# A channel shuffle on one core: the second tile cut from 8 to 4 KB a partition, the last raised from 16 to 20

## The chip, the cores and the metric

The kernel runs on one core of a Trainium2 chip. The metric is the device time of one execution in microseconds; lower is better. The time before is the median of three runs.

## The reference

The input is a float32 array of 16 x 64 x 64 x 256. The 256 channels of each pixel form 8 groups of 32. The output holds the same numbers with the two indices of the channel exchanged:

```python
def reference(x, groups):
    batch, h, w, c = x.shape
    channels_per_group = c // groups
    x = x.reshape(batch, h, w, groups, channels_per_group)
    x = x.transpose(0, 1, 2, 4, 3)
    return x.reshape(batch, h, w, c).astype(np.float32)
```

Nothing is calculated. Each pixel is one row of 256 x 4 bytes = 1 KB, read once, permuted inside the row, and written once: 67.11 MB in and 67.11 MB out.

## The kernel before, in words

The 65,536 rows are cut along the pixels into 15 slots, listed in `_SLOTS` (line 12). A slot is one input tile and one output tile in SBUF, with 128 partitions. The number in the list is the count of rows that each partition holds; a row is 1 KB, so the number is also the KB a partition. The first slot is cut once more, into two pieces of 4 and 8 rows, which share the slot's two buffers and are loaded, permuted and stored apart from each other. In this text each piece is called a tile: the first has 4 KB a partition, the second 8, the third 28, then come twelve of 38, and the last has 16. The sum is 512 rows a partition, times 128 partitions.

All buffers have the size of the biggest slot, 38 KB a partition. There are two input buffers (`_IN_BUFS`, line 13) and three output buffers (`_OUT_BUFS`, line 14), used in turn by slots.

For each slot three things happen, in program order:

- Line 55: SyncE (SP in the profile) issues a DMA for each piece, from HBM to the input tile. Partition p gets a contiguous stretch of rows, so one partition's part is one contiguous run on both sides. A load waits until the copies that read its buffer two slots earlier are over. The profile calls SP's queue q1.
- Line 57: VectorE (DVE) copies each piece from the input tile to the output tile. The permutation is in the access pattern: `(i g j)` is read as `(i j g)`. A copy waits for its load, and for the stores of the slot three before it, which hold the output buffer.
- Line 61: ScalarE's queue (ACT) issues the store of each piece after its copy. The profile calls this queue q10. ScalarE calculates nothing.

The schedule is manual, so each engine's instructions stand in the order in which the loop writes them. Nothing else is on the three queues. TensorE is not used, and GpSimd only sets four constants at the start.

Of the kernel before, what the change touches and what calls it, by code (L numbers as in the profile page):

```python
# [1 line left out]

# [4 lines left out]


F32 = mybir.dt.float32
P = 128  # L10

_SLOTS = [[4, 8], [28]] + [[38]] * 12 + [[16]]
_IN_BUFS = 2
_OUT_BUFS = 3


@with_exitstack
def kernel(
    ctx: ExitStack,
    tc: tile.TileContext,  # L20
    x: bass.AP,
    groups: bass.AP,
    out: bass.AP,
):
    nc = tc.nc
    b, h, w, c = x.shape
    G = int(groups)
    CPG = c // G
    assert G * CPG == c
    assert sum(map(sum, _SLOTS)) * P == b * h * w  # L30
    biggest = max(map(sum, _SLOTS))

    x_flat = x.rearrange("b h w c -> (b h w c)")
    out_flat = out.rearrange("b h w c -> (b h w c)")

    in_pool = ctx.enter_context(tc.tile_pool(name="in_pool", bufs=_IN_BUFS))
    out_pool = ctx.enter_context(tc.tile_pool(name="out_pool", bufs=_OUT_BUFS))

    def rows(flat, first, q):

        return flat[first * c : (first + P * q) * c].rearrange("(p f) -> p f", p=P)

    ctx.enter_context(tc.manual_schedule(engines=None))
    first = 0
    for parts in _SLOTS:
        in_tile = in_pool.tile([P, biggest * c], F32, name="in_tile")
        out_tile = out_pool.tile([P, biggest * c], F32, name="out_tile")
        at = 0
        pieces = []
        for q in parts:  # L50
            pieces.append((q, first, slice(at * c, (at + q) * c)))
            first += P * q
            at += q
        for q, start, cols in pieces:
            nc.sync.dma_start(out=in_tile[:, cols], in_=rows(x_flat, start, q))  # L55
        for q, start, cols in pieces:
            nc.vector.tensor_copy(  # L57
                out=out_tile[:, cols].rearrange("p (i j g) -> p i j g", j=CPG, g=G),
                in_=in_tile[:, cols].rearrange("p (i g j) -> p i j g", g=G, j=CPG),
            )  # L60
            nc.scalar.dma_start(
                out=rows(out_flat, start, q), in_=out_tile[:, cols]
            )


# [1 line left out]
_INS = ['x', 'groups']  # L67
_OUTS = [((16, 64, 64, 256), 'float32')]

_NUMBERS = {'groups': 8}  # L70


# [26 lines left out]
```

## Time and profile before

| What | Value |
|---|---|
| Time, median of 3 runs | 316.07 us (316.06 to 316.1) |
| Span of the profiled execution | 314.4 us |
| VectorE: 16 copies | 119.0 us |
| VectorE idle ahead of its copies, put down to loads | 179.4 us |
| A copy of 38 KB a partition | 8.79 us (x12) |
| Copies of 4, 8, 16, 28 KB a partition | 1.09, 2.02, 3.87, 6.57 us |
| DMA packets | 4608, in 32 DMAs |

The profile is of one execution. Its span runs from the first to the last instruction on the core; the times of the runs also hold what lies around it. "DMA packets" are the records of the 16 DMA engines: each packet is one piece of a transfer on one engine. A queue's share of 16 engines is the time its packets took, summed, over 16 times the span or the stretch asked for. Because loads and stores run on the same 16 engines, the two queues' shares add up, and a sum near 100% says that the engines have no free time.

The profile lists a DMA's time from issue to landing. It contains the time that the DMA stood behind others in its queue, so it is not the time of the transfer itself: the twelve loads of 38 KB a partition took a median of 37.0 us each and the stores 42.6, although together they pass in less than 314 us.

### The profile page before, as it was taken

How to read it: one execution, taken by the hardware profiler on the slowest of the kernel's cores; microseconds unless marked ns; L12 is line 12 of the kernel's file. 1: busy time of each engine (PE TensorE's matmuls, PEld its weight loads, DVE VectorE, ACT ScalarE, POOL GpSimd, SP SyncE). 2: the span in 40 equal slices, each digit the busy share in tenths (PEclk: the TensorE clock that was granted, in tenths of full speed). 3: DMA queues.
4: the chain of work that ended last, by engine and by line, in shares of the span. 5: the costliest groups of instructions: out<-in, count | busy, mean ns of one | idle time of the engine just before them, and what ended most of it. 6: DMA issues, size and time to landing. Idle time of an engine off the chain costs nothing.

```text
span 314.4 us, 132 instructions
## 1 busy us (share of the span) xinstructions
DVE 119.0 (38%) x16; POOL 0.2 (0%) x4
## 2 busy tenths in 40 slices
DVE  2081907309109109019028028037046055065400
POOL 0000000000000000000000000000000000000000
DMA  7999999999999999999999999999999999999997
GB/s 317 405 441 416 435 416 483 401 465 406 450 421 446 426 436 436 401 470 396 475 396 475 396 470 401 470 401 470 401 450 421 446 426 436 436 417 450 429 421 321
DMA packets 4608, 134.22 MB, mean 427 GB/s; under 512 B 512, under 2 KB 512, under 8 KB 768
## 3 DMA queue, kind: packets, MB, share of 16 engines
q1 hardware_dynamic: 2304, 67.11, 49.8%
q10 hardware_dynamic: 2304, 67.11, 49.4%
HBM read 67.11 MB, written 67.11 MB: 427 GB/s over the span
## 4 chain that ended last, share of the span: by engine, by line
DMA 76%; DVE 19%; issue 0%; SPq 0%; DVEq 0%
DMA in_tile<-in_x_dram 76%; DVE out_tile L57 19%; SPq L55 0%; DVEq L57 0%
## 5 line engine op out<-in xcount | busy, mean ns | idle before, releaser
L57 DVE COPY out_tile<-in_tile 128x9728 f32<-128x9728 f32 (+4 forms) x16 | 119.0, 7440 | 179.4 <-DMA in_tile<-in_x_dram 179.4
L80 POOL MEMSET const-uint8-127<- 128x1 uint8 x1 | 0.1, 103 | 0.0
L80 POOL MEMSET const-bfloat16-1.0<- 128x1 bf16 x1 | 0.1, 102 | 0.0
L80 POOL MEMSET const-float32-1.0<- 128x1 f32 x1 | 0.1, 100 | 0.0
L80 POOL MEMSET const-float32-0.0<- 128x1 f32 x1 | 0.1, 99 | 0.2 <-issue 0.2
## 6 DMA issues: line engine op xcount, KB each, us to landing
in_tile<-in_x_dram SPq DMA_DIRECT2D x12, 4864.0 KB, 37.0
out_dram<-out_tile ACTq DMA_DIRECT2D x12, 4864.0 KB, 42.6
in_tile<-in_x_dram SPq DMA_DIRECT2D x1, 3584.0 KB, 14.7
out_dram<-out_tile ACTq DMA_DIRECT2D x1, 3584.0 KB, 30.9
in_tile<-in_x_dram SPq DMA_DIRECT2D x1, 2048.0 KB, 30.4
out_dram<-out_tile ACTq DMA_DIRECT2D x1, 2048.0 KB, 15.2
in_tile<-in_x_dram SPq DMA_DIRECT2D x1, 1024.0 KB, 5.4
out_dram<-out_tile ACTq DMA_DIRECT2D x1, 1024.0 KB, 25.0
```

The costliest lines, as they stand in the source:

```text
L57: nc.vector.tensor_copy(out=out_tile[:, cols].rearrange("p (i j g) -> p i j g", j=CPG, g=G), in_=in_tile[:, cols].rearrange("p (i g j) -> ...
L80: nc = _bacc.Bacc("TRN2", target_bir_lowering=False, num_devices=1)
```

## The change

The second tile gets 4 rows a partition in place of 8, and the last tile 20 in place of 16. The sum stays 512, and every tile in between keeps its size but begins 4 x 128 rows earlier in the arrays.

```diff
-_SLOTS = [[4, 8], [28]] + [[38]] * 12 + [[16]]
+_SLOTS = [[4, 4], [28]] + [[38]] * 12 + [[20]]
```

The number of loads, copies and stores, their order on each engine and the buffers stay as they are. The second copy has 128 x 1024 elements in place of 128 x 2048, and the last one 128 x 5120 in place of 128 x 4096.

## The prediction

> **What bounds the kernel now.** I read the page's table of slices and its list of queues first, because the page shows only two consumers of time, VectorE copies and DMA.
>
> ```profile
> span 314.4 us, 132 instructions
> DVE 119.0 (38%) x16; POOL 0.2 (0%) x4
> ...
> DMA  7999999999999999999999999999999999999997
> ...
> DMA packets 4608, 134.22 MB, mean 427 GB/s; under 512 B 512, under 2 KB 512, under 8 KB 768
> ...
> q1 hardware_dynamic: 2304, 67.11, 49.8%
> q10 hardware_dynamic: 2304, 67.11, 49.4%
> ```
>
> The DMA row holds a 9 in 38 of 40 slices, with a 7 at either end; VectorE works 38% of the span. The two queues (q1 carries the loads that SP issues, q10 the stores that ACT issues) keep the 16 DMA engines busy for 49.8 + 49.4 = 99.2% of the span: 0.992 x 314.4 = 311.9 us. Only 2.5 us are not packets. So the sum is one over packets, not over waits.
>
> The chain of waits tells another story at first sight, and it is the trap of this page:
>
> ```profile
> 264.01 30.41 DMA in_tile<-in_x_dram
> 294.42 0.03 issue
> 294.45 0.05 DVEq L57
> 294.50 0.04 issue
> 294.54 3.87 DVE out_tile L57
> ```
>
> These rows (start, length, what) end at 298.4 with the last copy, 16 us short of the span's end, as if load, copy and store of the last tile stood in line. The listing does not show the stores that were already queued. The issue list, asked between 270 and 290 us, gives the next-to-last store: issued at 286.96, 21.8 us to landing, so landed at 308.8. The last store, issued at 298.45, had to stand behind it on the same queue and landed 15.2 us after issue, at 313.6. Its copy was over some 10 us before its turn came.
>
> Where are the 2.5 us without packets? I cut the span into stretches (the columns: stretch, length, VectorE, GpSimd, TensorE clock, DMA share, GB/s):
>
> ```profile
> 0.00:2.00 2.00, 0.00 (x0) 0.20 (x4) 1.00 0.18 23
> ...
> 16.00:32.00 16.00, 8.39 (x2) 0.00 (x0) 1.00 1.00 425
> 32.00:36.00 4.00, 4.00 (x1) 0.00 (x0) 1.00 1.01 397
> ...
> 100.00:250.00 150.00, 55.91 (x7) 0.00 (x0) 1.00 1.00 432
> ...
> 312.00:314.40 2.40, 0.00 (x0) 0.00 (x0) 1.00 0.27 116
> ```
>
> The first 2 us hold 0.18 of a full DMA, so 1.6 us are empty; the last 2.4 hold 0.27, so 1.75 are empty. (Together a little over 2.5, because the packets' recorded times overlap a little elsewhere: shares of 1.01 and more.) In between there is no gap, only two rough stretches, 16 to 36 us, where the rate is 425 and 397 in place of 432.
>
> **The change part by part.** The counts stand: 16 loads, 16 copies, 16 stores, the same 67.11 MB each way. A queue's 2304 packets are 16 DMAs x 16 engines x 9, and the 512 packets under 512 B are 32 DMAs x 16 engines; so on each engine a DMA is 8 data packets, one for each of its 8 partitions, and one tiny one. The second tile's packets go from 8 KB to 4 KB, the last one's from 16 to 20 KB. Prices of a packet come from stretches in which one kind is alone on a queue (packets, MB, share of 16 engines):
>
> ```profile
> q1 hardware_dynamic: 70, 0.29, 100.2%
> ```
>
> between 2.6 and 3.3 us, all 4 KB: 0.7 x 16 x 1.002 / 70 = 0.1603 us.
>
> ```profile
> q10 hardware_dynamic: 112, 0.92, 19.7%
> ```
>
> between 20 and 31 us, all 8 KB: 11 x 16 x 0.197 / 112 = 0.3096 us.
>
> ```profile
> q10 hardware_dynamic: 80, 1.31, 101.8%
> ```
>
> between 309 and 312 us, all 16 KB: 3 x 16 x 1.018 / 80 = 0.6108 us. The trace has no 20 KB packet. From 4 to 16 KB a KB costs (0.6108 - 0.1603) / 12 = 0.0375 us; from 16 to 38 KB it is nearly the same: between 100 and 200 us the queues hold 100.7% with 1247 - 128 = 1119 data packets, 100 x 16 x 1.007 / 1119 = 1.440, and (1.440 - 0.6108) / 22 = 0.0377. So 20 KB: 0.6108 + 4 x 0.0376 = 0.761 us, whichever slope one takes.
>
> Removed on each queue: 8 x (0.3096 + 0.6108) = 7.363 us. Added: 8 x (0.1603 + 0.761) = 7.370 us. Over two queues the change costs +0.01 us. If I take 8 KB from the loads alone between 3.9 and 5.8 us (97 packets at 101.0%, 0.3165 us, cut packets at the edges counted whole), it is 2 x 8 x -0.007 = -0.10 us. I take the first price, and keep -0.10 to +0.01.
>
> Small transfers: the row above has 4 KB packets back to back, at 100.2% of the engines and 0.1603 us each, which is what the sum uses. A rule speaks against the change: the Trainium skill, DMA: Bandwidth & Descriptors, section Bandwidth, says to batch DMAs to at least 1 MiB, and the change halves a DMA of exactly 1 MiB. By the fixed 2.0 us plus bytes over 436 GB/s in that page's section Anatomy of one DMA, an estimate gives 4.4 us for the second load before and 3.2 after, 6.8 and 8.0 for the last one: again a sum of zero, since the number of DMAs stands; only a reading in which the 2.0 us are newly exposed would make it cost.
>
> Start, step by step. SP issues three loads with no wait, at 0.73, 1.15 and about 1.6 us. The second is 8 x (0.3096 - 0.1603) = 1.19 us shorter, so its copy starts at 6.61 - 1.19 = 5.42 (the first copy ends at 5.15), takes 1.09 as the first one does in place of 2.02, and ends at 6.51 in place of 8.63. The second store on ACT and the fourth load on SP go out 2.1 us earlier; SP and ACT have nothing else queued behind these than the next load and store. All this is worth nothing: the load queue is full without the fourth load until the third lands at 16.34 (now 15.15), and the stores that start earlier take turns from loads. The cover is the third load's 28 KB packets; without it the 2.1 us would be a gain.
>
> The third load's packets must be there 1.19 us earlier. The first load's packets start between 1.7 and 1.8 us, 1.0 after its issue; so the third's are due at about 2.6, and are wanted when the second load is done, about 4.7 on the earliest engine. Cost 0. The upper bound is the slowest case the trace has: the first store was issued at 5.19 and its first packet is seen between 9.0 and 9.2 us, 3.9 later, though behind the loads' packets. At that delay the third load would begin at 5.5, a hole of up to 0.8 us. I take 0, the case of an issue on an empty queue.
>
> Buffers. The copy of each tile also waits for the store three tiles back. All 179.4 us of idle VectorE are put down to loads; the first tile's stores land at 8.66 + 25.0 = 33.7, and the copy that reuses their buffer starts at 49.11. 15 us cover it; nothing moves by more than 2.1. Loads: SP issues each one when a copy ends (57.9, for one), some 13 us before the load in front lands (71.2).
>
> End. The last load starts 1.19 us earlier and is 8 x 0.150 = 1.20 longer, so it lands at 294.4 as before. VectorE: the copy of 16 KB a partition takes 3.87, and 4 KB more cost 2.02 - 1.09 = 0.93; so 4.80, and the store is issued at 299.4 in place of 298.45. The next-to-last store is now done at about 308.8 - 1.2 = 307.6. With 1.0 us from issue to first packet that leaves 7 us where 9 stood; the copy's 0.93 is hidden. The last store drains 8 x 0.761 = 6.09 in place of 4.89, 1.20 later, which is what the queue in front gave up.
>
> Sum: 314.4 + 0.01 = 314.4 for the span; the runs' median is 316.07, 1.6 above the profiled span, and that offset (launch and end outside the span) has no cause to move. 316.07 + 0.01 = 316.1 us.
>
> **Rivals.** (1) Tail exposed, slower. If the chain of waits were right, the last tile would stand alone: +0.93 of copy and +1.20 of drain: 316.07 + 2.13 = 318.2. It decides once the last store comes to its queue after the one in front is done. For it: that the chain ends there. Against it: 7 us of slack. 2 in 100.
>
> (2) Hole at the start, slower. The third load's packets come later than 3.1 us after their issue (1.6 + 3.1 = 4.7): up to 0.8 us, 316.9. For it: the 3.9 us of the first store. Against it: 1.0 us of the first load. 7 in 100, of which half passes 0.2%.
>
> (3) Smoother start, faster. The rough stretches cost 16 x (432 - 425)/432 = 0.26 and 4 x (432 - 397)/432 = 0.32 us. The second store's 8 KB packets lie in the first of them; were both to go with the smaller packets, 316.07 - 0.58 - 0.10 = 315.4. For it: from 36 us on the rate is full. Against it: 4 KB packets are dearer for each byte, and the loads beside the second store are the same. 6 in 100. The opposite, a new slow stretch of that size somewhere, gives 316.6; another 4 in 100.
>
> (4) Shorter fill, faster. If the first stores were what the end waits for, 2.1 us earlier gives 314.0. Against it: DMA is full from 2 us on. 1 in 100.
>
> **How the numbers follow.** No change, 316.1 with its own range 315.8 to 316.4 (-0.10 and half of the rough 0.58 either way): 80 in 100. The runs of before differ by 0.04 us; 0.2%, 0.63 us, is what I take as the least a measurement can tell. Slower by more: (1), half of (2) and a little of the opposite of (3): 0.07. Faster by more: (4), half of (3), rounded up: 0.05. Within: 0.88. The range for 8 in 10 reaches to the far side of (3) and most of (2): 315.4 to 316.8.
>
> **What would show it.** Queue shares that again sum to about 99.2%; second copy at 5.4 us with 1.09, last one 4.8 long with its store issued near 299.4 and 14 us to landing; an unbroken row of 9s. Wrong if a stretch near 4 to 6 us has a share well under 1 (rival 2), if stores' queue is empty between 300 and 309 (rival 1), or if the stretch from 100 to 250 us leaves 432 GB/s: then packets do not cost what their size says.

## The result, and the profile after

The changed kernel is slower: 318.07 us (median of 9 runs, 316.79 to 319.72) against 316.10 for the kernel before (9 runs in turn with them, 316.05 to 316.75). The ratio is 1.0054, with a 95% interval of 1.0035 to 1.0073. That is outside the predicted range, and on the other side of 0.2%. The spread is new too: the runs of before lie within 0.7 us, those of the changed kernel within 2.9. (Medians here are over all runs; ratios leave out executions over 1.5% above the fastest of the same kernel, and so do the readings of profiles below, which is why two of the experiments, e1 and g1, have none.)

The page of the changed kernel, of an execution that took 318.74 us, to be laid beside the lines that the prediction showed:

```profile
span 317.0 us, 132 instructions
...
DMA  8999999999999999999999999999999999999995
...
DMA packets 4608, 134.22 MB, mean 423 GB/s; under 512 B 512, under 2 KB 512, under 8 KB 1024
...
q1 hardware_dynamic: 2304, 67.11, 49.5%
q10 hardware_dynamic: 2304, 67.11, 49.0%
```

The packets and bytes are as many as before, and 256 more packets are under 8 KB: the second tile's. Their time is (0.495 + 0.490) x 317.0 = 312.2 us of 16 engines, against 311.9 before. So the packets cost 0.3 us more (0.4 when their recorded times are summed one by one, 312.40 against 311.99), and the span grew by 2.6. The DMA row has 9s in 38 slices, and the last digit has gone from 7 to 5.

The stretches at the end (stretch, length, VectorE, GpSimd, clock, DMA share, GB/s), first of the kernel before, then of the changed one:

```profile
312.00:313.30 1.30, 0.00 (x0) 0.00 (x0) 1.00 0.51 214
313.30:314.40 1.10, 0.00 (x0) 0.00 (x0) 1.00 0.00 0
```

```profile
312.00:313.80 1.80, 0.00 (x0) 0.00 (x0) 1.00 0.59 250
313.80:316.20 2.40, 0.00 (x0) 0.00 (x0) 1.00 0.04 17
```

In the changed kernel 2.4 us follow in which the share is 0.04, less than 1/16 = 0.06. The DMA view of 314.1 to 316.5 us says what moves there (40 slices: busy tenths, then GB/s):

```profile
DMA  0007000000000007000000000000000000000000
GB/s 0 0 0 341 0 0 0 0 0 0 0 0 0 0 0 341 0 0 0 0 0 0 0 0 0 0 0 0 0 0 0 0 0 0 0 0 0 0 0 0
DMA packets 3, 0.04 MB, mean 17 GB/s; under 512 B 1, under 2 KB 1, under 8 KB 1
```

Three packets one behind the other: two of 20 KB and a tiny one. That is a single engine, which finishes its share of the last store alone. The trace's landings, one for each engine, agree: the last store lands on 15 engines between 313.25 and 313.97 us, and on the sixteenth at 316.15. Before, all 16 land between 313.21 and 313.62. So of the 2.53 us between the two last landings, 316.15 - 313.97 = 2.2 are one engine's lateness and 0.35 are the other fifteen.

How it began can be read from the third copy. In the timeline (start, length, what, idle time before it) of the changed kernel:

```profile
16.34 6.56 DVE L57 COPY out_tile<-in_tile 128x7168 f32<-128x7168 f32 x1 [9.99 <-DMA in_tile<-in_x_dram]
```

It starts at 16.34, as it did before (16.36), although there are 4 KB less to load ahead of it; the prediction had its load landing at 15.15. The landings say why: on the first engine the third load is there at 14.86, on the last at 16.32, 1.46 us apart. Before they were 0.42 apart (15.92 to 16.34). A copy waits for the last of 16.

The lateness is there from the first packet of that load. On the engine that later ends alone it starts between 5.1 and 5.2 us, and no other packet starts in that stretch (packets, MB, share of 16 engines):

```profile
q1 hardware_dynamic: 1, 0.03, 146.8%
```

A packet counts with its whole time where it starts, so this one took 0.1 x 16 x 1.468 = 2.35 us, where a 28 KB packet usually takes 1.06. The first packets of seven other engines took 0.26 to 0.89 us too long, those of the remaining eight none. The first store's packets begin at 9.4 us, so no store was in the way.

The difference lasts. The DMA view of 100 to 112 us, before and after:

```profile
DMA  0295008920099000990009800292009920099000
GB/s 0 130 1686 259 0 0 389 1556 130 0 0 1297 778 0 0 0 1297 778 0 0 0 1686 389 0 0 130 1816 130 0 0 1038 908 130 0 0 1297 778 0 0 0
```

```profile
DMA  9025993099920989209892099039990299902989
GB/s 1167 0 130 259 778 908 130 0 519 519 908 130 0 778 389 778 130 0 778 389 778 130 0 778 1167 0 130 519 519 908 0 130 519 649 778 0 130 778 389 778
```

A packet is counted where it starts. Before, the 16 engines start theirs in clumps 1.44 us apart, the length of a 38 KB packet, with nothing between: all load, then all store. After, the clumps are smeared, and some engines load while others store. I call the state of before "in step". (For single engines I linked each packet record to the one that starts where it ends.)

### The profile page after: what moved, and what is told of

It reads as the page before. It is cut to its first block, busy times and chain, and to the rows that moved or that the text cites. A ratio compares the mean times of both kernels' runs of the same rounds, so it can differ in the third digit from the quotient of the medians.

```text
span 317.0 us, 132 instructions
## 1 busy us (share of the span) xinstructions
DVE 120.1 (38%) x16; POOL 0.2 (0%) x4
## 2 busy tenths in 40 slices
DMA packets 4608, 134.22 MB, mean 423 GB/s; under 512 B 512, under 2 KB 512, under 8 KB 1024
## 4 chain that ended last, share of the span: by engine, by line
DMA 76%; DVE 19%; issue 0%; SPq 0%; DVEq 0%
DMA in_tile<-in_x_dram 76%; DVE out_tile L57 19%; SPq L55 0%; DVEq L57 0%
## 5 line engine op out<-in xcount | busy, mean ns | idle before, releaser
L57 DVE COPY out_tile<-in_tile 128x9728 f32<-128x9728 f32 (+3 forms) x16 | 120.1, 7504 | 180.6 <-DMA in_tile<-in_x_dram 180.5
```

The lines of the kernel that those rows point to most:

```text
L57: nc.vector.tensor_copy(out=out_tile[:, cols].rearrange("p (i j g) -> p i j g", j=CPG, g=G), in_=in_tile[:, cols].rearrange("p (i g j) -> ...
```

## The experiments

Two theories at the start. A: the third load's packets, wanted 1.2 us earlier, come apart on the engines at the start. B: the 20 KB tile at the end makes the late engine. A third one, C, puts it on the shifted rows. The first four kernels change only the list of tiles.

```diff
-_SLOTS = [[4, 4], [28]] + [[38]] * 12 + [[20]]
+_SLOTS = [[4, 4], [32]] + [[38]] * 12 + [[16]]    e1_start
+_SLOTS = [[4, 8], [24]] + [[38]] * 12 + [[20]]    e2_end
+_SLOTS = [[4, 6], [28]] + [[38]] * 12 + [[18]]    e3_mid
+_SLOTS = [[12], [28]] + [[38]] * 12 + [[16]]      e4_single
```

> Only the second tile goes from 8 to 4 KB a partition; the third takes the 4 KB (32), the last stays at 16. Theory A (the loss comes from the start: the third load's packets begin at 4.7 us in place of 5.9, are slow there, and one DMA engine falls out of step and ends alone some 2 us after the others): slower like the changed kernel, 317 to 319 us with runs over 1 us apart, and a last engine alone after the others. Theory B (the 20 KB tile at the end makes the straggler): 316.1 us, all engines ending within 0.5 us. Theory C (the shifted rows, 4 x 128 earlier, meet memory worse): 316.1 us too, since from the fourth tile on the rows are those of before.

Measured: ratio 1.0052 (1.0038 to 1.0065), the whole loss, with no change at the end. B and C fall as its main cause.

> The second tile keeps 8 KB a partition, the third gives up 4 KB (24), the last has 20. Theory A (start): 316.1 us, runs within 0.7 us, engines ending together. Theory B (20 KB tile at the end): 317 to 319 us. Theory C (shifted rows from the fourth tile on): 317 to 319 us.

Measured: 316.73 us, ratio 1.0025 (1.0012 to 1.0038). Less than half of the loss, but not none, with the third load only 0.51 us apart. Theory A had 316.1. In the trace the first store's packets begin at 8.8 to 9.3 us on half of the engines and at 9.8 to 10.3 on the others.

> Second tile 6 KB, last one 18: half of the change. Theory A: the third load begins 0.6 us earlier than before; if the loss grows with the lead, some 317 us with a spread between runs; if there is a step (the third load's packets are ready at a fixed moment), either 316.1 or as the changed kernel. Theory B: half of the loss, 317 us.

Measured: 317.82 us, 1.0043 (1.0025 to 1.0061), with runs from 316.01 to 318.68. The third load lands 0.50 us apart, yet the first store's packets begin at 8.7 and 9.0 us on two engines and at 9.7 to 10.0 on the other fourteen, one 28 KB packet later.

> One first tile of 12 KB a partition in place of 4 and 8; the rest as before. The second load (28 KB) begins about 5.9 us, as the third did before, but was issued 0.5 us earlier, and the first store comes some 3 us later and with 12 KB packets. Theory A, in the form that the large load's packets are late: 316.1 us with engines in step. Theory A, in the form that small store packets beside large load packets put the engines out of step: 316.1 or a little less, and no rough stretch between 8 and 36 us. If early stores were worth anything: 317 us or more.

Measured: 317.82 us, 1.0049 (1.0026 to 1.0071). All four are slower than before, and none gives a stable time. So the kernel of before is not one of many equals: it is a special case. In its trace all 16 engines begin the first store between 9.1 and 9.75 us, at one boundary between load packets. This suggests a theory D: what counts is that the engines are in step, and the moment at which the first store arrives decides it. It can be tested with the tiles of before and nothing moved but that moment:

```diff
+            if start == 0:
+                nc.vector.tensor_copy(
+                    out=out_tile[:, : 2 * c].rearrange("p (i j g) -> p i j g", j=CPG, g=G),
+                    in_=in_tile[:, : 2 * c].rearrange("p (i g j) -> p i j g", g=G, j=CPG),
+                )
             nc.vector.tensor_copy(
```

> The tiles of before; VectorE first copies 2 of the first tile's 4 rows once more, so the first store goes out about 0.6 us later (5.8 in place of 5.2 us) and nothing else moves: the second copy still starts when its load lands at 6.6. Theory D (the kernel of before is fast because all 16 DMA engines take the first store's packets at the same boundary between two 28 KB load packets, which are 1.06 us long, and so do loads together and stores together to the end; any other moment splits them in two groups, and out of step some engine is slowed and ends alone): half a packet later splits them: 316.5 to 318.5 us, runs over 1 us apart, first store landing over 1 us apart on the engines. Theory A (the third load's early packets alone make the loss; here they are where they were): 316.1 us. Bytes alone: 316.1.

> As the one above with all 4 rows copied twice: the first store about 1.09 us later, one 28 KB packet's time (1.06). Theory D: the engines meet the next boundary together again: 316.1 us, runs within 0.7 us. Theory A: 316.1. If any delay or any more work on VectorE did the harm, it would be slower than the one above.

Measured: 318.17 us for 2 rows (5 runs, 317.78 to 318.78; ratio 1.0063, 1.0051 to 1.0075), and 316.13 for 4 rows (ratio 1.0004, 0.9996 to 1.0013). The timeline of the kernel with 2 rows:

```profile
4.67 1.09 DVE L62 COPY out_tile<-in_tile 128x1024 f32<-128x1024 f32 x1
5.80 0.38 ACTq L66 DMA_DIRECT2D out_dram<-out_tile  x1
6.58 2.02 DVE L62 COPY out_tile<-in_tile 128x2048 f32<-128x2048 f32 x1 [0.82 <-DMA in_tile<-in_x_dram]
```

The first store goes out at 5.80 in place of 5.19; the second copy still starts when its load lands (6.58; before 6.61). Bytes, tiles, loads and every later wait are those of before, and 0.6 us of delay on a 512 KB store costs 2 us at the end of the kernel. Twice the delay costs nothing in most runs (7 of 12 between 316.02 and 316.14), though at 317.32 us, the longest, its profile shows a split too (first store's packets on 10 engines at 10.2 to 10.8 us, on 6 at 11.4 to 11.8). In the profile of 2 rows, three engines begin the first store at 9.5 to 9.6 us and the others from 10.2 us on, about one 28 KB packet later. This speaks for theory D. Theory A had 316.1 us for both, so it is not the whole cause.

If the step is all, an order that leaves an engine no choice should be immune. SP issues the stores too (the lines that put the loads into a function `load`, called for the first two slots ahead of the loop, are left out here):

```diff
-            nc.scalar.dma_start(
+            nc.sync.dma_start(
                 out=rows(out_flat, start, q), in_=out_tile[:, cols]
             )
+        if s + 2 < len(slots):
+            loaded.append(load(s + 2))
```

> The tiles of the changed kernel, but SP issues the stores too, in the order load 0, load 1, then for each slot its store and the load two slots on: one queue, so a DMA engine has no choice between loads and stores. Theory D: no split is possible, engines stay in step: 315.5 to 316.3 us, runs within 0.7 us, in spite of 4 and 20 KB tiles. Theory A: the third load still starts at 4.7 us: 317 to 319 us, runs apart. A cost of one queue (a load that has to stand behind a store that is not yet allowed) would show as holes in the DMA row, and over 320 us.

> The same one queue with the tiles of before. Theory D: as the one above within 0.3 us, so that the tile sizes no longer matter. Theory A: 1 to 2 us faster than the one above.

Measured: 321.9 us (1.0182, 1.0164 to 1.0199) with the changed kernel's tiles, 322.26 (1.0185, 1.0172 to 1.0198) with those of before. The tile sizes no longer matter, as D said, but the level is 6 us too high, and not for holes. The page of e7 and its stretches at the end:

```profile
span 321.4 us, 118 instructions
...
DMA  7999999999999999999999999999999999999982
...
q1 hardware_dynamic: 4608, 134.22, 97.5%
```

```profile
312.00:317.00 5.00, 0.00 (x0) 0.00 (x0) 1.00 0.54 229
317.00:321.40 4.40, 0.00 (x0) 0.00 (x0) 1.00 0.04 19
```

The row is full until the engines run out one after the other, over 5.4 us. In e8 they are 0.40 us apart when the second store lands at 20.6 and 5.3 at the end. One queue does not keep engines in step; that part of D is wrong.

Can the changed kernel be brought back into step by the moment of its first store? The edit is that of e5 with 1 to 4 rows, on the changed kernel's tiles.

> The changed kernel's tiles; VectorE first copies 1 of the first tile's 4 rows once more, so the first store goes out about 0.39 us later (and, since VectorE has no free time there, the second store and the fourth load too, which have 8 us of cover). Theory D (step of the DMA engines): the profile of the changed kernel shows 13 engines with the first store's packet at 9.4 to 9.9 us and 3 at 10.8, so the store comes just at the border between two 28 KB packets; 0.39 later more engines are pushed to the later packet: still split, 317 to 319 us. Theory A (the third load starts at 4.7 us in place of 5.9): 317 to 318.5 us.

> The same with 2 rows, about 0.63 us later. Theory D: most engines take the later packet; 316.3 to 317.5 us. Theory A: 317 to 318.5 us as with any delay.

> The same with 3 rows, about 0.86 us later. Theory D: all engines have passed the border and take the later packet together: the best of the four, 316.1 to 316.7 us, runs within 0.7 us, although the tile sizes are those of the changed kernel. Theory A: 317 to 318.5 us.

> The same with 4 rows, about 1.09 us later, a whole 28 KB packet (1.06). Theory D: split again as the changed kernel without a delay, 317 to 319 us, unless the border is sharper than the spread of the engines; so among the four delays there is a best and a worst over 1 us apart. Theory A: all four within 0.5 us of each other.

Measured: 317.72, 318.10, 318.76 and 318.26 us; ratios 1.0044, 1.0049, 1.0074 and 1.0073, with intervals that overlap. No delay helps, and D is wrong here: it had 3 rows as the best, and their median is the highest. A, which had four times within 0.5 us of each other, is nearer, though the medians are 1.04 us apart. In the profiles with 1, 3 and 4 rows the third load lands 1.80, 1.45 and 1.37 us apart, and the engines were over 1.4 us apart after its first packet, before any store's packet. With 2 rows it lands 0.46 us apart; that profile is of the fastest of its runs (316.91 us), and yet it is slower than before.

What pulls it apart? The first two kernels below change the tiles (`[[4, 4, 4], [28]] ... [[16]]` and `[[8, 4], [28]] ... [[16]]`); the other two send the third tile's store ahead of the first two tiles' on ACT, so that no store is in flight before 23 us:

```diff
-            nc.scalar.dma_start(
-                out=rows(out_flat, start, q), in_=out_tile[:, cols]
-            )
+            held.append((start, q, out_tile[:, cols]))
+        if parts is not _SLOTS[0]:
+            for start, q, piece in held[-1:] + held[:-1]:
+                nc.scalar.dma_start(out=rows(out_flat, start, q), in_=piece)
+            held = []
```

> The 12 KB of the first slot in three tiles of 4 KB, the rest as before: the second tile has 4 KB as in the change, but the 28 KB packets start at 5.9 us as before and the first store goes out at 5.2 us as before. Theory A (it is the large packets' start at 4.7 us that pulls the engines apart): third load landing within 0.6 us on all engines, 316.1 to 316.5 us, runs mostly within 0.7 us. If the 4 KB second tile (a second store with 4 KB packets, one more DMA) does it: 317 to 319 us.

> First tile 8 KB, second 4 KB, the rest as before: the 28 KB packets start at 5.9 us as before; the first store goes out some 2.0 us later than before (first load 1.2 later, its copy 0.9 longer), about two 28 KB packets. Theory A: third load landing within 0.6 us on all engines; the time then depends on where 2.0 us falls: 2 x 1.06 is near a whole number of packets, so 316.1 to 317 us. If the 4 KB second tile does it: 317 to 319 us.

> The changed kernel's tiles, but ACT issues the third tile's store first and the first two tiles' stores behind it, so no store is in flight before about 23 us. If the early issue of stores pulls the third load's packets apart: that load lands within 0.6 us on all engines. Theory A (loads alone): it lands over 1 us apart as in the changed kernel, and the time is 317 to 319 us. If engines that are in step at 23 us are all that is needed and 4.7 us has no part: 316.1.

> The same hold with the tiles of before: third load landing within 0.6 us; the first store meets 38 KB load packets (1.44 us) at 23 us. Theory A and D: between 316.1 (met together) and 318 (split), and not slower than the one above. Early stores worth something: slower than before by what the stores start later; bytes alone say nothing is lost: 316.1.

Measured: g3 318.86 us (1.0087, 1.0072 to 1.0101), although its 28 KB packets begin at 5.9 us; its third load, now 4 KB, is already 1.36 us apart, and the 28 KB load is 1.23. So large packets behind are not needed to pull a third load apart, and the half of A that blames them falls. g4 317.08 us (1.0024, 1.0014 to 1.0033), 0.88 apart. g1 is 1.0058 (1.0034 to 1.0082, from three of its eight runs), with runs from 316.84 to 330.0, g2 1.0034 (1.0018 to 1.0050) with the third load 0.41 apart. Holding the stores back does not help: g1 loses what the changed kernel does, and g2 loses too. Nor are early stores the cause of the start's disorder in the changed kernel: its engines are 1.7 us apart after the first packet of the third load, before any store's packet.

> Second tile 12 KB, last one 12; first tile and first store as before. The third load's 28 KB packets start some 1.2 us later than before (7.1 us), 0.13 us more than one packet. If engines in step at the first store are what counts, and only a third load wanted before about 5.3 us disturbs them: third load landing within 0.6 us on all engines, 316.1 to 316.7 us. If 4 + 8 KB is a lucky case and any other size splits the engines: 317 to 319 us.

> First tile 2 KB, second 6, the last one 20: 8 KB in sum as in the changed kernel, no tile of 4 KB. If the moment at which the third load's packets are wanted (4.7 us) pulls them apart: third load landing over 1.2 us apart, 317 to 319 us. If it is the 4 KB second tile: within 0.6 us, and 316.1 to 317.5 us, depending on where the earlier first store falls.

The tiles are `[[4, 12], [28]] ... [[12]]` and `[[2, 6], [28]] ... [[20]]`. Measured: h1 316.58 us (1.0021, 1.0010 to 1.0032), third load 0.45 apart. h2 316.41 us (1.0030, 1.0009 to 1.0050), third load 0.29 apart, 7 of 12 runs at 316.05 to 316.43 and the others up to 319.08. The last profile, of a run of 316.1 us, is the most telling one: 8 KB in sum ahead of the third tile and 20 KB at the end, as in the change, and in step.

```profile
span 314.3 us, 132 instructions
...
q1 hardware_dynamic: 2304, 67.11, 49.7%
q10 hardware_dynamic: 2304, 67.11, 49.4%
```

```profile
DMA  0009900099000950099200990009900098000920
GB/s 0 0 0 1038 1038 0 0 0 1556 519 0 0 0 1816 259 0 0 519 1427 130 0 0 908 1167 0 0 0 1167 908 0 0 0 1686 389 0 0 0 1946 130 0
```

The clumps between 100 and 112 us are those of the kernel before, and the span is 314.3. Its third copy:

```profile
14.53 6.55 DVE L57 COPY out_tile<-in_tile 128x7168 f32<-128x7168 f32 x1 [7.48 <-DMA in_tile<-in_x_dram]
```

Its 28 KB packets begin from 4.72 us on, those of the changed kernel from 4.68. So a third load wanted at 4.7 us need not come late, and A in this form does not hold for this run; the five runs of h2 that took 317.16 to 319.08 us have no profile, so how they began is not shown. The rows from the fourth tile on are those of the changed kernel, so the shift of C alone costs nothing here. The landings of the profiles of all kernels with two queues but e1 and g1, in us:

| Kernel | First tiles, KB | Third load apart | Last store: first engine | last engine | Span |
|---|---|---|---|---|---|
| before | 4, 8, 28 | 0.42 | 313.21 | 313.62 | 314.4 |
| h2_26 | 2, 6, 28 | 0.29 | 313.18 | 313.51 | 314.3 |
| e2_end | 4, 8, 24 | 0.51 | 313.74 | 314.42 | 315.2 |
| g2_hold_before | 4, 8, 28 | 0.41 | 313.83 | 314.37 | 315.2 |
| g4_84 | 8, 4, 28 | 0.88 | 313.70 | 314.45 | 315.3 |
| e4_single | 12, 28 | 1.12 (the 28) | 313.26 | 314.08 | 315.0 |
| f2_after_d2 | 4, 4, 28 | 0.46 | 313.24 | 314.32 | 315.1 |
| e6_delay4 | 4, 8, 28 | 0.53 | 313.38 | 314.73 | 315.6 |
| h1_412 | 4, 12, 28 | 0.45 | 313.01 | 315.40 | 316.2 |
| e5_delay2 | 4, 8, 28 | 0.56 | 313.29 | 315.20 | 316.0 |
| e3_mid | 4, 6, 28 | 0.50 | 313.31 | 315.28 | 316.1 |
| f4_after_d4 | 4, 4, 28 | 1.37 | 313.37 | 315.80 | 316.6 |
| g3_444 | 4, 4, 4, 28 | 1.23 (the 28) | 313.23 | 315.97 | 316.8 |
| changed | 4, 4, 28 | 1.46 | 313.25 | 316.15 | 317.0 |
| f3_after_d3 | 4, 4, 28 | 1.45 | 313.26 | 316.17 | 317.0 |
| f1_after_d1 | 4, 4, 28 | 1.80 | 314.01 | 317.69 | 318.5 |

The first engine ends at 313.0 to 314.0 whatever the tiles. The span is the last engine's landing plus 0.8 to 0.9 us in every row. What differs most is how late the last engine is.

## Why the prediction was wrong

**The step that failed** is "So the sum is one over packets, not over waits." That sum is right for the 16 engines together: their packets took 312.2 us after and 311.9 before, and the run of h2 with the same 20 KB tile ends at 314.3. But it makes a mean of 16 queues, and the kernel ends with the last. The profile of before gave no sign of a distance between engines, because there it was 0.4 us; I read as a property of the kernel what e5 shows to hang on the moment of one store.

**Point by point.** The price of the tiles: right. (The factor -0.007 ahead of -0.10 should be -0.006; the product stands. The 2.0 us that the prediction takes from the Trainium skill, DMA: Bandwidth & Descriptors, section Anatomy of one DMA, are given there for DMAs that GpSimd issues; SP and ACT issue these, no run here shows the figure, and no term of the sum rests on it.) The last copy took 4.78 us (4.80 was predicted), and the profile of h2 shows that the 20 KB tile costs nothing where the engines are in step. The second copy started at 5.27 and the second store went out at 6.39, 0.15 earlier than worked out. The third load's landing: wrong, 16.32 in place of 15.15, by the engine that came last. Its cost, taken as 0 between bounds of 0 and 0.8 us as "a hole of up to 0.8 us", was the seed: its first packet took 2.35 us on the engine that later ends alone, in place of 1.06. So the disturbance was 1.3 us on that engine and up to 0.9 on seven others, where rival (2) had 0.8 on all, and it was slow packets, not a hole. The term that the sum lacked altogether is what follows: this engine fell back further, by load packets that took up to 0.66 us too long, until about 135 us. Counting packets over 40 ns above the median of their size, it lost 3.3 us in all and the other fifteen 1.0 to 1.8; in e3, e5, f4 and h1, too, the engine that ends last lost 2.5 to 3.0 us. Among the copies nothing is wrong before the third; behind it each copy waits for the engine that is late.

**The end.** The last load landed at 295.74 (294.4 was predicted) and the last store was issued at 300.7, still 6.5 us ahead of the first engine that was free for it. Rival (1), the tail exposed, is rejected: no engine waited for that copy. Rival (3) had the rough stretches smoothed. Their rates did rise, from 425 and 397 to 432 and 419 GB/s, but between 8 and 16 us the rate fell from 470 to 411, and the kernel became slower. The sign of rival (2), a share well under 1 between 4 and 6 us, did not come although the load was late, and the rate between 100 and 250 us, the sign that packets cost more than their size says, stayed: 434 GB/s after and 432 before. A mean over engines cannot show one of them. The rows, first one of before, then those of the changed kernel:

```profile
8.00:16.00 8.00, 0.63 (x1) 0.00 (x0) 1.00 1.12 470
```

```profile
4.00:6.00 2.00, 1.82 (x2) 0.00 (x0) 1.00 1.30 475
...
8.00:16.00 8.00, 0.00 (x0) 0.00 (x0) 1.00 0.99 411
16.00:32.00 16.00, 9.49 (x2) 0.00 (x0) 1.00 1.01 432
32.00:36.00 4.00, 4.00 (x1) 0.00 (x0) 1.00 1.06 419
...
100.00:250.00 150.00, 55.22 (x7) 0.00 (x0) 1.00 1.00 434
```

**What stays open.** Why 4 + 4 KB pulls the third load apart. In the profiles above and those of e7 and e8 it lies over 1.2 us apart in 6 of 7 kernels that begin with 4 + 4 KB, and within 0.56 in all nine that begin with 2 or 4 KB and then 6 KB or more. The slowest of the sixteen first packets of the third load took 0.6 to 1.3 us too long in the six of those seven whose third load has 28 KB, and at most 0.3 in the nine. Neither the stores nor the size of the packets behind explains it. The moment alone does not either, by h2; but h2 is the only one of the nine in which the third load is wanted at 4.7 us, so the size of the second tile and that moment are told apart by a single profile. One profile of each kernel is little for a thing that varies from run to run: e3, e5 and h1 are in step in the third load and out of it later.

## What to carry to other kernels

Where DMA bounds a kernel, compare the engines with each other: when does each of the 16 land the last transfer? A share under 1/16 in the last microseconds is less than one engine's full work, so look there for one that works alone. And a time that repeats closely (the kernel before took 316.0 to 317.1 us in all its runs here) may hang on one moment: shift one early transfer by half a packet before taking such a kernel as the base for pricing edits.

## What the runs showed of the hardware that was not expected

Where engines fall back, it is loads that are slowed, hardly ever stores. From 36 us on, in 15 kernels with two queues (all but that of before and the two whose profiles are left out), 295 of 20,147 load packets of 38 KB took over 40 ns longer than 1439, and 15 of 23,040 store packets did. Being out of step is not enough for it: in e4 each store lands 2.0 us apart on the engines from 30 to 280 us, with 1 such load packet. About 100 of the 295 follow directly upon the tiny packet that ends a store on the same engine, a place where only some 2,170 of the 20,147 stand: 4.7% of those are slow, against 1.1% of the others. That is an association; no run took it apart.

One queue was slower than two here: the same bytes on SP's queue alone, in the order load, store, load, took 321.9 and 322.3 us, 1.8% more, with a full DMA row and engines that fell back further from one transfer to the next (e8: 0.40 us apart at 20.6 us, 2.5 at 54, 3.6 at 147, 5.3 at the end).

A delay does not simply add to the time. 0.6 us on the first store became 2 us at the end (e5), and 1.1 us became nothing in most runs (e6).
